# Decay projection of a gated linear attention: one fp32r product over 96 stacked rows instead of one fp32 product over 16

## Chip, cores and metric

The kernel runs on one core of a Trainium2 chip. The metric is the device time of one execution in microseconds. The time before is the median of three runs, 2531.12 us (2529.14 to 2533.62).

## The reference, cut to what matters

A two-layer encoder trunk works on 1040 positions (16 meta tokens and 1024 frames) of width 1024. Each layer has an input projection, a gated linear attention (GLA) with four heads, a softmax attention with a forget gate (FoX) with eight heads, an output projection, and a gated convolutional FFN. The change concerns the per-key decay of the GLA:

```python
gq, gk, gv, gr, glr, fq, fk, fv, ff = jnp.split(xn @ w_in[i], cuts, axis=-1)
log_a = jax.nn.log_sigmoid((glr @ w_alpha_up[i] + b_alpha[i])) / GLA_TAU
...
log_b = jnp.cumsum(log_a, axis=3)          # inside chunks of 64 frames
u = einsum(k * jnp.exp(log_end - log_b), v)  # state increment of a chunk
```

`glr` has 16 columns (the low rank) and `w_alpha_up[i]` is 16 x 256, so the product has a contraction of 16 and gives one decay for each of 4 x 64 keys and each position.

## The kernel before, in words

Activations lie transposed: features on partitions, the 1040 positions along the free axis, which is cut into three chunks of 400, 384 and 256 columns (`CH`).

**Large products.** TensorE is used in fp32r, a 4-byte format of less precision. To keep fp32 accuracy each operand is split into a high part (ScalarE copies it to fp32r) and a low part (VectorE or GpSimd subtracts the high part from the source). `mm3` (L222 to L224) makes a product of three passes: high x high, low weight x high activation, high weight x low activation. Weights are loaded by SP in pieces and split in `weights` (L189 on ScalarE, L191 on VectorE, or on GpSimd in the FoX stage).

**Start of a layer.** `attention` (L886) first makes the GLA. Its head makes three products chunk by chunk: the remainder tile (the 16 low-rank columns in rows 0 to 15, the eight forget-gate columns in rows 32 to 39), the keys `gk` and the first values `gv`. In layer 0 the input is still being split at that time (L297, L298) and squared for the norm (L310 on ScalarE, summed by L311 on VectorE or GpSimd). For each chunk the sum of squares is finished by an fp32 product with ones (L322, `ssq`), and VectorE and ScalarE make the reciprocal root from it (L328, L277, L278, L279 to L281). Then the chunk of the three products is evacuated: `ev_rem` (L909 to L921) adds and scales the remainder tile into `t` (L912 to L914), copies its first 16 rows to `rem` (L915) and makes the log-sigmoid of the forget gates (L346 to L350); `gk` is scaled by L413, the value tiles by L424. After the last chunk the forget gates are summed by a scan (L919) and stored (L921).

**The decay.** When the keys of a pair of heads are complete, `gla_decay` (L455 to L477) is queued behind the next product. For each chunk it makes `z`, an fp32 product of the weights `wau` (16 x 128 of the pair) with 16 rows of `rem` (L462), and its log-sigmoid into the tiles `B` and `A` (L346 to L350). A scan along the chunks (L466), a subtraction from the end of the chunk (L470, L472), an exponential (L476) and a multiplication into the keys (L477) follow. The kernel has two pairs of heads and two layers, so `gla_decay` runs four times, with three `z` products each. `z` uses the PSUM tag `S`, which has three banks; in the head these also hold the products of the third chunk until L413 and L424 evacuate them.

**The steps of the GLA.** `gla_steps` (L480 on) transposes the decayed keys (L491), copies them (`kd`, L492), multiplies them with the values (`u`, L506), updates the states (L513, L515), multiplies the queries with the states (`o`, L523), normalises (L529 to L538, tile `on`) and transposes back (L545). Between these it runs pieces of the next large products (`fill`). The steps of pair 0 run beside the products of pair 1, those of pair 1 beside the first FoX products; `gla_decay` of pair 1 falls into the steps of pair 0. The values are transposed to natural order by `to_natural` (L447, L450).

**Order of the work.** In the attention a scheduler orders the instructions of each engine by its own cost estimates, so a cheaper or an added instruction can move its neighbours. In the FFN the order of TensorE is written out by hand. Every engine takes its own queue in order. GpSimd's queue also issues DMAs, among them the load of `wau` (L904) and the store of the forget gates (L921). Tiles of a pool with the same tag share a buffer: `lc` and `A` share one.

Of the kernel before, what the change touches and what calls it, by code (L numbers as in the profile page):

```python
# [10 lines left out]
F32 = mybir.dt.float32  # L11
F32R = mybir.dt.float32r
BF16 = mybir.dt.bfloat16
AF = mybir.ActivationFunctionType
ALU = mybir.AluOpType
# [6 lines left out]
DEPTH = 2  # L22
META = 16
T = META + SEQ
# [32 lines left out]
class Slots:  # L57
# [6 lines left out]
    def add(self, pool, n, prefix):  # L64
        ids = [(pool, f"{prefix}{i}") for i in range(n)]
        self.free += ids
        return ids
# [68 lines left out]
class Kern:  # L136
# [318 lines left out]
    def gla_decay(self, lyr, p, gp, pp, g):  # L455
        nc = self.nc
        rem, gk = g["rem"], g["gk"]
        A = gp.tile([128, T], F32, tag="A", name="A")
        B = gp.tile([128, T], F32, tag="B", name="B")
        for c0, n in CH:  # L460
            z = pp.tile([128, 512], F32, tag="S", name="z")
            nc.tensor.matmul(z[:, :n], self.wau[:, lyr, 128 * p:128 * p + 128], rem[0:16, c0:c0 + n],  # L462
                             start=True, stop=True)
            self.log_sigmoid(B[:, c0:c0 + n], A[:, c0:c0 + n], z[:, :n], self.v(lyr, V_BA, p),
                             self.ones[:, 0:1])
        nc.vector.tensor_tensor_scan(out=A[:], data0=self.reset[:], data1=B[:], initial=0.0,  # L466
                                     op0=ALU.mult, op1=ALU.add)
        Ar = A[:, META:T].rearrange("p (c t) -> p c t", t=64)
        Br = B[:, META:T].rearrange("p (c t) -> p c t", t=64)
        nc.vector.tensor_tensor(out=Br, in0=Ar[:, :, 63:64].to_broadcast([128, 16, 64]), in1=Ar,  # L470
                                op=ALU.subtract)
        nc.vector.tensor_tensor(out=B[:, 0:META], in0=A[:, META - 1:META].to_broadcast([128, META]),  # L472
                                in1=A[:, 0:META], op=ALU.subtract)
        g["dec"] = dec = gp.tile([128, 16], F32, tag="dec", name="dec", bufs=2)
        nc.scalar.activation(dec[:], Ar[:, :, 63:64].rearrange("p c t -> p (c t)"), AF.Exp, scale=1.0 / 16)
        nc.scalar.activation(B[:], B[:], AF.Exp, scale=1.0 / 16)  # L476
        nc.vector.tensor_tensor(out=gk[:, :T], in0=gk[:, :T], in1=B[:], op=ALU.mult)  # L477
# [408 lines left out]
    def attention(self, lyr, nm, hsrc, chunks, feed):  # L886
        tc, nc, s = self.tc, self.nc, self.slots
        with tc.tile_pool(name=f"aps{lyr}", bufs=2, space=PSUM, reuse_waits="tile") as pp2, \
# [7 lines left out]
            with tc.tile_pool(name=f"gla{lyr}", bufs=1, reuse_waits="tile") as gp:  # L896
                nm["tp"] = gp
                fd = feed(self.wm[lyr, M_REM])
                self.reset = gp.tile([128, T], BF16, name="reset")
                nc.gpsimd.memset(self.reset[:], 1.0)  # L900
                nc.gpsimd.memset(self.reset[:, 0:1], 0.0)
                nc.gpsimd.memset(self.reset[:, META:T].rearrange("p (c t) -> p c t", t=64)[:, :, 0:1], 0.0)
                self.wau = gp.tile([16, DEPTH, 256], F32, name="wau")
                nc.gpsimd.dma_start(self.wau[:], self.wau_d)  # L904
                rem = gp.tile([128, T], F32, tag="rem", name="rem")
                lc = gp.tile([128, T], F32, tag="A", name="lc")
                lr = slice(32, 40)

                def ev_rem(ps, c0, n):  # L909
                    r = self.norm_scale(nm, pp, c0, n)  # L910
                    t = gp.tile([40, 400], F32, tag="rt", name="rt", bufs=2)[:, :n]
                    nc.scalar.copy(t, ps[64:104])  # L912
                    nc.vector.tensor_tensor(out=t, in0=ps[0:40], in1=t, op=ALU.add)
                    nc.vector.tensor_tensor(out=t, in0=t, in1=r[0:40], op=ALU.mult)  # L914
                    nc.scalar.copy(rem[0:16, c0:c0 + n], t[0:16])  # L915
                    self.log_sigmoid(rem[lr, c0:c0 + n], lc[lr, c0:c0 + n], t[lr],
                                     self.v(lyr, V_BF, 0, lr), self.ones[lr, 0:1])
                    if c0 + n == T:
                        nc.vector.tensor_tensor_scan(out=lc[lr, :], data0=self.ones[lr, 0:1].to_broadcast([8, T]),  # L919
                                                     data1=rem[lr, :], initial=0.0, op0=ALU.mult, op1=ALU.add)  # L920
                        nc.gpsimd.dma_start(self.cd[:], lc[lr, :])  # L921
                work = Work()
                add = lambda tiles: [self.add_tile(work, pp, src, nm["x"], CH, ev) for src, ev in tiles]
                g = [{"rem": rem}, {"rem": rem}]
                tiles = [(self.wm[lyr, M_REM], ev_rem)] + self.gla_products(lyr, 0, gp, pp, nm, g[0])
                self.head(tiles[:3], pp, nm, fd)
                if fd:
                    fd["end"]()
                add(tiles[3:])
                work.drain()  # L930
                self.flush()
                add(self.gla_products(lyr, 1, gp, pp, nm, g[1]))
                self.gla_steps(lyr, 0, gp, pp, g[0], lambda us: work.run(us * 1.6))
                work.drain()
                self.flush()
                self.fox_products(lyr, 0, work, gp, pp, nm, qs[0])

                coming = {"src": self.wm[lyr, M_FQ + 1], "slots": None}
                work.boxes.append(coming)
                self.gla_steps(lyr, 1, gp, pp, g[1], lambda us: work.run(us * 1.3))  # L940
                work.drain()
                self.flush()
# [759 lines left out]
def layout(x, meta_tokens, attn_norm, w_in, w_alpha_up, b_alpha, b_forget, gla_norm, fox_norm, w_out,  # L1702
           ffn_norm, w_up, conv_w, conv_b, w_down, final_norm):
    hT0 = np.concatenate([meta_tokens, x[0]], axis=0).T.reshape(KD, 128, T)
    gq, gk, gv, gr, glr, fq, fk, fv, ff = np.split(w_in, np.cumsum([256, 256, 512, 512, 16, 512, 512, 512]), axis=2)
    zero = lambda n: np.zeros((DEPTH, D, n), w_in.dtype)
    rem = np.concatenate([glr, zero(16), ff, zero(88)], axis=2)
    up = w_up.reshape(DEPTH, D, 2, NFF, 128).transpose(0, 1, 3, 2, 4).reshape(DEPTH, D, 2 * NFF * 128)
    cols = np.concatenate([gk, gq, gv, gr, rem, fq, fk, fv, w_out, up], axis=2)
    wm = cols.reshape(DEPTH, KD, 128, N_M, 128).transpose(0, 3, 2, 1, 4)  # L1710
    wd = w_down.reshape(DEPTH, NFF, 128, KD, 128).transpose(0, 3, 2, 1, 4)
    vec = np.zeros((128, V_FIN + 8), w_in.dtype)
    for l in range(DEPTH):
        b = l * NV
        for off, a in ((V_AN, attn_norm[l]), (V_FN, ffn_norm[l]), (V_BA, b_alpha[l]),
                       (V_CW, conv_w[l].reshape(-1)), (V_CB, conv_b[l]), (V_GN, gla_norm[l]),
                       (V_XN, fox_norm[l])):
            t = a.reshape(-1, 128).T
            vec[:, b + off:b + off + t.shape[1]] = t
        vec[32:40, b + V_BF] = b_forget[l]  # L1720
    vec[:, V_FIN:] = final_norm.reshape(KD, 128).T
    wau = w_alpha_up.transpose(1, 0, 2)
    return {"hT0": hT0, "wm": wm, "wd": wd, "vec": vec, "wau": wau}


# [23 lines left out]
```

## Time and profile before

| | |
|---|---|
| median of three runs | 2531.12 us |
| the profiled execution | 2528.19 us |
| its span, first to last instruction | 2526.4 us |
| mean granted TensorE clock | 0.996 |
| `z` products L462 | 12, in 24 records |

A row of the timeline gives the start in us from the span's start, the duration, the engine, the line, the operation with output <- input and shape, the count, and in brackets the idle time of the engine before it and what ended it. A row of the chain of waits gives start, length and what the end of the span was waiting for at that time; there TensorE's instructions stand with the step that they take in its stream. A row of a group gives line, engine, names, shapes and count, then busy us and mean ns of one, then the idle time before them. A row of the waits gives who waited for whom, us in total, times, and the longest. PEld is the load of weights into TensorE.

### The profile page before, as it was taken

What the parts mean: (1) busy time and instruction counts of PE and PEld (TensorE: products, weight loads), DVE (VectorE), ACT (ScalarE), POOL (GpSimd) and SP (SyncE); (2) the same over time, 40 slices, a digit from 0 to 9 for tenths busy, and PEclk for the clock granted to TensorE, in tenths of its full rate; (3) what the DMA queues carried; (4) which work ended last, traced back from release to release, by engine and by line L of the source; (5) the groups of instructions that cost most, each with busy time, mean ns of one, the idle gap of its engine ahead of it and who ended that gap; (6) DMA issues with size and microseconds to landing.
All of it is one profiled execution on the core that took longest, in us unless ns stands there. A gap on an engine that the chain in (4) does not pass through costs nothing.

```text
span 2526.4 us, 47023 instructions
## 1 busy us (share of the span) xinstructions
PE 2488.1 (98%) x18454; PEld 2386.5 (94%) x18454; DVE 1767.5 (70%) x3515; ACT 1274.1 (50%) x2731; POOL 381.4 (15%) x561
## 2 busy tenths in 40 slices
PE   9999999999999999999999999999999999999998
PEld 8989999999999999999999899999999999997786
DVE  8656777769877777853666666777797777777545
ACT  7346666645544445641443466665464444455412
POOL 1023433110000000100200333431100000001002
PEclk9999999999999999999999999999999999999999
DMA  3232124342322224763312222243432222258622
GB/s 131 68 87 73 50 89 132 116 139 76 118 81 81 81 76 138 196 176 102 105 56 70 74 80 69 67 147 110 145 92 93 76 82 83 77 158 191 183 75 73
DMA packets 117933, 259.75 MB, mean 103 GB/s; under 512 B 14816, under 2 KB 32480, under 8 KB 117712
## 3 DMA queue, kind: packets, MB, share of 16 engines
q1 hardware_dynamic: 93408, 181.74, 23.1%
q0 software_dynamic: 22432, 72.71, 10.4%
q8 instruction: 144, 2.36, 0.4%
q10 hardware_dynamic: 1872, 2.31, 0.3%
q14 instruction: 77, 0.63, 0.1%
HBM read 176.11 MB, written 67.81 MB: 97 GB/s over the span
## 4 chain that ended last, share of the span: by engine, by line
PE 83%; DVE 10%; ACT 4%; issue 1%; DMA 1%; SPq 0%; DVEq 0%; ACTq 0%
PE up L224 11%; PE up L222 11%; PE up L223 11%; PE mm L222 7%; PE mm L224 7%; PE mm L223 7%; PE down L222 5%; PE down L223 5%; PE down L224 5%; PE av L721 3%; PE tr L695 2%; DVE S L662 1%; PE S L659 1%; PE wo L222 1%; PE wo L224 1%
## 5 line engine op out<-in xcount | busy, mean ns | idle before, releaser
L224 PE MATMUL up<-x,hi 128*128 128x260 f32 (+1 forms) x2464 | 698.0, 283 | 2.8 <-DVE x L1090 2.8
L222 PE MATMUL up<-x,hi 128*128 128x260 f32 (+1 forms) x2464 | 698.2, 283 | 2.4 <-ACT x L1089 2.4
L223 PE MATMUL up<-x,lo 128*128 128x260 f32 (+1 forms) x2464 | 697.1, 283 | 0.0
L224 PEld LDWEIGHTS up<-x,hi 128*128 128x128 f32 x2464 | 466.8, 189 | 5.1 <-DVE x L1090 4.8
L222 PEld LDWEIGHTS up<-x,hi 128*128 128x128 f32 x2464 | 465.7, 189 | 3.3 <-ACT x L1089 3.2
L223 PEld LDWEIGHTS up<-x,lo 128*128 128x128 f32 x2464 | 466.0, 189 | 0.1
L1066 DVE TENSOR_TENSOR lo<-raw,hi 128x512 fp32r<-128x512 f32 x364 | 247.5, 685 | 172.0 <-ACT hi L1065 172.0
L222 PE MATMUL mm<-xh,hi 128*128 128x348 f32 (+4 forms) x1056 | 363.6, 344 | 0.0
L224 PE MATMUL mm<-xl,hi 128*128 128x348 f32 (+4 forms) x1056 | 339.6, 322 | 0.0
L223 PE MATMUL mm<-xh,lo 128*128 128x348 f32 (+4 forms) x1056 | 338.9, 321 | 0.0
L1065 ACT CAST hi<-raw 128x512 fp32r<-128x512 f32 x364 | 224.8, 620 | 141.5 <-PE up L224 93.0
L222 PEld LDWEIGHTS mm<-xh,hi 128*128 128x128 f32 x1056 | 199.6, 189 | 5.9 <-issue 5.3
L223 PEld LDWEIGHTS mm<-xh,lo 128*128 128x128 f32 x1056 | 199.5, 189 | 0.4 <-issue 0.3
L224 PEld LDWEIGHTS mm<-xl,hi 128*128 128x128 f32 x1056 | 198.4, 188 | 0.4 <-issue 0.3
L189 ACT CAST hi<-raw 128x512 fp32r<-128x512 f32 (+2 forms) x168 | 97.3, 580 | 183.2 <-PE down L224 108.0
L223 PE MATMUL down<-ah,lo 128*128 128x260 f32 (+1 forms) x528 | 169.1, 320 | 0.0
L222 PE MATMUL down<-ah,hi 128*128 128x260 f32 (+1 forms) x528 | 168.6, 319 | 0.0
L224 PE MATMUL down<-al,hi 128*128 128x260 f32 (+1 forms) x528 | 168.4, 319 | 0.0
L674 ACT ACTIVATE P<-S,m 116x460 f32<-116x460 f32 (+2 forms) x224 | 124.7, 561 | 71.6 <-DVE m L662 67.6
L337 DVE TENSOR_TENSOR PT<-tr,PT 116x464 fp32r<-116x464 f32 (+3 forms) x240 | 122.8, 514 | 47.0 <-ACT PT L336 45.4
L1048 DVE TENSOR_TENSOR raw<-raw,raw 128x512 f32<-128x512 f32 x198 | 129.4, 683 | 18.1 <-DMA raw<-in_wd_dram 15.6
L1279 POOL DMA_DIRECT2D actd<-cv x44 | 23.6, 535 | 763.0 <-DVE cv L1278 742.1
(285 smaller groups left out, 5615.6 us busy)
## 6 DMA issues: line engine op xcount, KB each, us to landing
raw<-in_wm_dram SPq DMA_DIRECT2D x326, 256.0 KB, 2.7
raw<-in_wd_dram SPq DMA_DIRECT2D x64, 256.0 KB, 3.8
actd<-cv POOLq DMA_DIRECT2D x22, 520.0 KB, 3.0
actd<-cv POOLq DMA_DIRECT2D x22, 512.0 KB, 3.0
cb<-cd SPq DMA_DIRECT2D x16, 520.0 KB, 4.2
st<-actd SPq DMA_DIRECT2D x14, 520.0 KB, 5.0
st<-actd SPq DMA_DIRECT2D x14, 512.0 KB, 4.8
kA<-kA SPq DMA_DIRECT2D x24, 260.0 KB, 4.1
```

Of the source, the lines that this page charges most:

```text
L189: nc.scalar.copy(hi[:, :n, :], raw[:, :n, :])
L222: nc.tensor.matmul(ps, wh, xh[:, c0:c0 + n], start=first, stop=False, skip_group_check=more)
L223: nc.tensor.matmul(ps, wl, xh[:, c0:c0 + n], start=False, stop=False, skip_group_check=more)
L224: nc.tensor.matmul(ps, wh, xl[:, c0:c0 + n], start=False, stop=last, skip_group_check=more)
L337: nc.vector.tensor_tensor(out=lo, in0=src, in1=hi.bitcast(F32), op=ALU.subtract)
L659: nc.tensor.matmul(S[:rows, :n], q["qA"][e][:, qs], q["kA"][e][:, c0:k1], start=True, stop=False)
L674: nc.scalar.activation(P[:rows, :n], S[:rows, :n], AF.Exp, scale=-1.0, bias=m[:rows, nch - 1:nch], accum_out=(den if nch == 1 else d3[:row ...
L695: nc.tensor.transpose(tr[:w, 3 - j, :rows], P[:rows, o:o + w], id_)
L721: nc.tensor.matmul(av[:, a:b], w.rearrange("p a b -> p (a b)"), x, start=(t == ts[0] and part == 0 and i == 0), stop=(t == last and i == 1))
L1048: nc.vector.tensor_tensor(out=q[out][:, :nk, :], in0=q[a][:, :nk, :], in1=q[b][:, :nk, :], op=op)
L1065: nc.scalar.copy(hi[:, :nk, :], src[:, :nk, :])
L1066: nc.vector.tensor_tensor(out=lo[:, :nk, :], in0=src[:, :nk, :], in1=hi[:, :nk, :].bitcast(F32), op=ALU.subtract)
```

## The change

The product `z` keeps its shape and its place, and becomes a single fp32r product with a contraction of 96 rows. The rows are three groups of 32, of which 16 carry data: activations high, low, high, and weights high, high, low. One pass so adds the same three terms as `mm3`.

- `ev_rem` writes the three groups of `rz`: the high part by ScalarE (32 rows in place of 16), the low part by a subtraction on VectorE, the second copy of the high part by GpSimd.
- The host layout of `wau` holds the weights three times in 96 rows, and a layer loads its own part only. After the last chunk ScalarE copies the 96 x 256 weights to fp32r (`wz`), and VectorE replaces the last group by its low part.
- The forget gates keep their tile `rem`, which now shares the buffer of tag `B`; `rz` takes the buffer of tag `rem`.

```diff
@@ gla_decay
-            nc.tensor.matmul(z[:, :n], self.wau[:, lyr, 128 * p:128 * p + 128], rem[0:16, c0:c0 + n],
-                             start=True, stop=True)
+            nc.tensor.matmul(z[:, :n], self.wz[:, 128 * p:128 * p + 128], rem[:, c0:c0 + n], start=True, stop=True)
@@ attention
-                self.wau = gp.tile([16, DEPTH, 256], F32, name="wau")
-                nc.gpsimd.dma_start(self.wau[:], self.wau_d)
-                rem = gp.tile([128, T], F32, tag="rem", name="rem")
+                wau = gp.tile([96, 256], F32, name="wau")
+                nc.gpsimd.dma_start(wau[:], self.wau_d[:, lyr, :])
+                self.wz = wz = gp.tile([96, 256], F32R, name="wz")
+                rz = gp.tile([96, T], F32R, tag="rem", name="rz")
+                rem = gp.tile([128, T], F32, tag="B", name="rem")
...
-                    nc.scalar.copy(rem[0:16, c0:c0 + n], t[0:16])
+                    hi, lo, hi2 = (rz[a:a + 32, c0:c0 + n] for a in (0, 32, 64))
+                    nc.scalar.copy(hi, t[0:32])
+                    nc.vector.tensor_tensor(out=lo, in0=t[0:32], in1=hi.bitcast(F32), op=ALU.subtract)
+                    nc.gpsimd.tensor_copy(hi2, hi.bitcast(F32))
...
                         nc.gpsimd.dma_start(self.cd[:], lc[lr, :])
+                        nc.scalar.copy(wz[:], wau[:])
+                        nc.vector.tensor_tensor(out=wz[64:96, :], in0=wau[64:96, :], in1=wz[64:96, :].bitcast(F32),
+                                                op=ALU.subtract)
...
-                g = [{"rem": rem}, {"rem": rem}]
+                g = [{"rem": rz}, {"rem": rz}]
@@ layout
-    wau = w_alpha_up.transpose(1, 0, 2)
+    wau = np.zeros((96, DEPTH, 256), w_in.dtype)
+    for a in (0, 32, 64):
+        wau[a:a + 16] = w_alpha_up.transpose(1, 0, 2)
```

In the changed kernel the new lines are L917 (high part), L918 (low part), L919 (second copy), L926 and L927 (weights); the scan of the forget gates is L923, and lines of `gla_decay` and `gla_steps` stand one lower than before (L462 keeps its number). The prediction names lines that both kernels have by their number before.

## The prediction

> **What bounds the kernel now.** I read the page first: span, busy shares, clock, chain.
>
> ```profile
> span 2526.4 us, 47023 instructions
> PE 2488.1 (98%) x18454; PEld 2386.5 (94%) x18454; DVE 1767.5 (70%) x3515; ACT 1274.1 (50%) x2731; POOL 381.4 (15%) x561
> PEclk9999999999999999999999999999999999999999
> GB/s 131 68 87 73 50 89 132 116 139 76 118 81 81 81 76 138 196 176 102 105 56 70 74 80 69 67 147 110 145 92 93 76 82 83 77 158 191 183 75 73
> PE 83%; DVE 10%; ACT 4%; issue 1%; DMA 1%; SPq 0%; DVEq 0%; ACTq 0%
> ```
>
> TensorE is busy for 98% of the span at the full granted clock, and 83% of the chain is its own work. So a microsecond taken from its stream is a microsecond off the end, unless another engine makes it wait at that place. The second view is therefore TensorE's waits. The place near the change that already waits is the products u of the GLA steps, for the transposed keys kd (0.9 us in two waits, one in each layer):
>
> ```profile
> PE u L506 <- DVE kd L492: 0.9, 2, 0.5
> ```
>
> The third view is the chain of waits cut to the places where the decay product z (L462) stands. It gives each instruction its real step in TensorE's stream, while the matmul durations of other views overlap each other. There are four sets of z: GLA pair 0 and pair 1, in each of two layers; each has three chunks (400, 384 and 256 columns).
>
> ```profile
> 47.16 0.18 PE mm L222
> 47.70 1.72 PE z L462 x4
> 49.44 0.67 PE z L462 x2
> 50.11 0.37 PE tr L450 x2
> 50.83 0.17 PE mm L224
> 89.66 1.94 PE z L462 x6
> 1301.38 1.94 PE z L462 x6
> 1310.11 0.12 PE mm L222
> 1342.92 1.94 PE z L462 x6
> ```
>
> The sets last 2.41 us (layer 0, pair 0: 47.70 to 50.11) and 1.94 us (the three others). A chunk is two records, since it is an fp32 product. The fp32r products beside them take one record and 0.18, 0.17 and 0.12 us for 400, 384 and 256 columns. The first set is longer because it waits inside:
>
> ```profile
> 48.52 0.29 PEld L462 LDWEIGHTS z<-rem,wau 16*128 16x128 f32 x2 [0.59 <-DVE gk L413]
> 49.41 0.29 PEld L462 LDWEIGHTS z<-rem,wau 16*128 16x128 f32 x2 [0.60 <-ACT lc L346]
> ```
>
> The second chunk waits for the evacuation of gk (L413) and the third for that of the first value tile (L424): z takes the PSUM banks that those free. In layer 0 VectorE's queue, and not TensorE, already sets the end of this set.
>
> **The change, part by part.**
>
> *TensorE, removed and added.* Twelve fp32 products become twelve fp32r products with 96 rows; the rows of a contraction do not lengthen it: the steps above are of products with 128 rows. A set then costs 0.18 + 0.17 + 0.12 = 0.47 us; I take 0.50, since entering another kind of product costs some hundredths. An unhindered set falls from 1.94 to 0.50: **1.44 us** saved. Four of them would be 5.8 us.
>
> *What the order of the built program says.* On SP the order is the same. On TensorE, VectorE and ScalarE it differs only in the GLA stage of each layer; the FoX and FFN stages are unchanged instruction for instruction. So nothing else needs pricing but the two GLA stages. Four kinds of work are added per layer: three subtractions L918 and one L927 on VectorE, one copy L926 on ScalarE (256 columns, 0.4 us by L915 below, and ScalarE is busy for half of the span), three copies L919 on GpSimd. L917 takes the place of L915 with twice the rows and the same columns.
>
> *Layer 0, pair 0.* VectorE's queue decides here. Its rows:
>
> ```profile
> 37.95 1.23 DVE L191 TENSOR_TENSOR lo<-raw,hi 128x512 fp32r<-128x512 f32 x1
> 39.10 0.54 DVE L281 SCALAR_TENSOR_TENSOR r<-ra,y 128x384 f32<-128x384 f32 x1
> 39.67 0.55 DVE L914 TENSOR_TENSOR rt<-rt,r 40x384 f32<-40x384 f32 x1
> 42.08 0.69 DVE L191 TENSOR_TENSOR lo<-raw,hi 128x512 fp32r<-128x512 f32 x1
> 43.02 0.42 DVE L913 TENSOR_TENSOR rt<-mm,rt 40x256 f32<-40x256 f32 x1 [0.25 <-ACT rt L912]
> 43.66 0.55 DVE L350 TENSOR_TENSOR rem<-rem,lc 8x384 f32<-8x384 f32 x1 [0.23 <-ACT lc L348]
> 44.91 0.42 DVE L328 TENSOR_SCALAR vv<-ssq 128x256 f32<-128x256 f32 x1
> 47.71 0.42 DVE L914 TENSOR_TENSOR rt<-rt,r 40x256 f32<-40x256 f32 x1
> 48.06 0.41 DVE L413 TENSOR_TENSOR gk<-mm,r 128x256 f32<-128x256 f32 x1
> 48.50 0.34 DVE L349 TENSOR_SCALAR rem<-rt,vec 8x256 f32<-8x256 f32 x1
> 48.87 0.90 DVE L424 TENSOR_TENSOR vt<-mm,r 128x256 f32<-128x256 f32 x2
> ```
>
> A subtraction of 32 rows is priced by L914, 40 rows of the same length: a step of 0.48 us at 400 and 384 columns, 0.38 at 256. Ahead of L281 come L918 (0.48) and L927 (0.4), and one L191 leaves (1.15, the slow one): L281 of the second chunk stays at about 39.1. Between it and L328 of the third chunk come L918 (0.48) and that L191 at its undisturbed step (0.61), 1.09 in all. The two waits on ScalarE (0.25 and 0.23) absorb 0.48 of it, and another 0.16 goes to smaller gaps: L328 starts about 0.45 late, at 45.36. From there the chain keeps its steps to L349, then L918 (0.38) stands ahead of L424. The first L424 ended near 49.37 (its pair is 0.90 from 48.87, and the third z loads at 49.41); now it ends near 49.37 + 0.45 + 0.38 = 50.20. The last z then ends at 50.20 + 0.05 + 0.12 = 50.37 in place of 50.11. **This set loses 0.25 us**: all that TensorE saves is given back to the wait. Waits of TensorE further ahead (xl of the third chunk and vt of the second each come later on VectorE) end before this one and are absorbed by it. Bounds: 0.3 gained if VectorE loses nothing up to L328, 1.1 lost if none of the added work finds slack.
>
> The third way to z is the GpSimd copy, which is not in the trace. It starts when the high part is there, which in layer 0 is 0.45 later than the end of L915 was:
>
> ```profile
> 48.16 0.40 ACT L915 COPY rem<-rt 16x256 f32<-16x256 f32 x1 [1.93 <-DVE rt L914]
> 1300.30 0.41 ACT L915 COPY rem<-rt 16x256 f32<-16x256 f32 x1 [1.93 <-DVE rt L914]
> L573 POOL TENSOR_TENSOR qA<-qt,qA 64x348 fp32r<-64x348 f32 x32 | 29.8, 933 | 25.7 <-ACT qA L572 24.0
> L839 POOL TENSOR_TENSOR cb<-cb,mask 116x116 f32<-116x116 f32 x128 | 58.8, 461 | 213.2 <-DVE m L662 152.9 <-DMA cb<-cd 26.9 <-DVE fa L279 11.5
> ```
>
> Its nearest rows are 0.46 us (116 columns, two inputs) and 0.93 (348 columns, two inputs); for 256 columns and one input I take 0.65, an estimate between them. It lands at 48.56 + 0.45 + 0.05 + 0.65 = 49.7, before 50.20, and costs nothing here; at 0.93 it still lands before it. The first copy (400 columns) stands in GpSimd's queue ahead of seven additions for the norm, the last five of which are these, with TensorE's ssq product that reads them:
>
> ```profile
> 34.09 4.54 POOL L311 TENSOR_TENSOR r<-r,sq 128x256 f32<-128x256 f32 x5 [0.78 <-ACT sq L310]
> 42.90 0.43 PE ssq L322 x2
> ```
>
> They end at 38.63 and are read at 42.90, so they have 4 us to spare and that copy is hidden.
>
> *Layer 1, pair 0.* VectorE has idle time ahead of this set, so only the last additions count:
>
> ```profile
> 1301.01 0.98 DVE L424 TENSOR_TENSOR vt<-mm,r 128x256 f32<-128x256 f32 x2
> 1303.32 0.37 PE tr L450 x2
> ```
>
> L918 pushes the first L424 from 1301.46 to 1301.84. GpSimd's copy ends at 1300.71 + 0.05 + 0.65 = 1301.4 (1301.7 at 0.93). The first two z take 1301.38 to 1301.78, the third starts at 1301.9 and ends at 1302.07, against 1303.32. **1.25 us gained** (0.6 to 1.45).
>
> *Pair 1, both layers.* The operands are old, so z itself waits for nothing and TensorE runs 1.44 us ahead. But it runs towards the wait for kd:
>
> ```profile
> 96.00 0.56 DVE vt L424
> 96.56 2.23 DVE A L466
> 100.78 0.48 DVE kd L492
> 101.30 0.89 PE u L506 x24
> ```
>
> TensorE came to u at 100.85 and waited 0.45. The new order puts seven 400-column products and one transpose (7 x 0.18 + 0.11 = 1.39 us) ahead of u, so TensorE comes to u at 100.80. On VectorE the new order is denser before the scan L466 (both L538 and all of L350 now stand ahead of it): counting steps from the first L349 I get the scan at 96.5 and kd at 101.6, against 101.26. Then u starts at 101.65, 0.35 later but with 1.39 more done: **1.05 us gained** in each layer. Bounds: 0.4 if kd slips by another 0.65, 1.9 if kd is there when TensorE comes.
>
> *Start.* The load of wau grows from 32 to 96 KB in layer 0, beside the loads on which the first products wait. At the 131 GB/s of the first slice, 64 KB are 0.5 us if they all stood in the way; I take 0.1.
>
> **Sum.** -0.25 + 1.25 + 2 x 1.05 - 0.1 = 3.0 us. The profiled execution took 2528.19 us (span 2526.4 and 1.8 around it); it would take 2525.2. The median of the runs shown is 2531.12, 2.9 above it, so I forecast 2531.1 - 3.0 = **2528.1 us**, 0.12% faster. A measurement of this kernel can tell about 0.2%, or 5.1 us, from no change, so this counts as within.
>
> **Rivals.**
>
> *A: the whole saving arrives.* kd is ready when TensorE comes, so the old waits go too (1.9 per layer), layer 1 pair 0 gives 1.4 and layer 0 nothing: 5.2 us, 2525.9. For it: the scan no longer stands behind the vt evacuation that TensorE released at 96.0. Against it: by my count VectorE is busy without a gap from 90.6 to 101.6. It decides from kd being 0.8 us earlier than I count.
>
> *B: GpSimd holds up VectorE, and the kernel is slower.* The trace shows the same L191 at 1.23 us beside GpSimd's additions and at 0.69 without them, so a copy on GpSimd can cost VectorE time. If each L919 costs VectorE its whole length at the high price (0.93), the three in layer 0 delay L424 by up to 2.8 us and the last in layer 1 by 0.9: 3.0 - 3.7 = -0.7, 2531.8. It decides from 0.75 us of delay per copy, four copies eating 3.0 us. Against it: two of the copies meet VectorE at work that reads PSUM or one small operand, and L191 lost 0.54 beside some five additions in a row.
> The Trainium skill (SBUF — State Buffer, Who interferes with whom) says that a VectorE instruction with two SBUF inputs contends with a GpSimd instruction that reads SBUF, and that the lock is held for the whole instruction. The 1.23 beside 0.69 agrees in direction; L918 has two SBUF inputs and L919 reads SBUF, so by that rule B is the case, with L918 of the third chunk waiting out its L919.
>
> *C: the fp32r product is no faster here* (96 rows in three groups, each half padded with zeros). Then only the added work is left: 0.25 + 0.4 + 0.1, about 2532. Against it stands every fp32r row above.
>
> **Chances.** Forecast 0.58, A 0.25, B 0.12, C 0.05. Most of A, and about one in seven of the forecast (scatter of a median: the runs shown go from 2529.1 to 2533.6), end faster by over 0.2%: 0.30. Part of B and C, where several delays meet, end slower by over 0.2%: 0.08. The rest, 0.62, lies within. Range: from the best ends of the terms (0.3 + 1.45 + 3.8 = 5.5 us gained, and 2 us of scatter) to the worst (-1.1 + 0.6 + 0.8 - 0.5 = -0.2, and 1.2 of scatter): 2523.6 to 2532.5.
>
> **What would show it.** Right: the z sets on the chain are 0.5 us in pair 1; the third z of pair 0 in layer 0 still waits on L424 near 50.2; u still waits for kd, 0.5 to 0.9 us; everything after the GLA stages keeps its durations and is only earlier. Wrong: z steps above 0.2 us (C); L918 or L191 much longer beside L919 (B); no wait at u (A); z waiting on GpSimd in layer 1; or a new TensorE wait at the transposes of on (L545 before), which I count at nothing because VectorE reaches them within 0.3 us.

## The result and the profile after

The changed kernel takes 2527.09 us (median of 22 runs, 2524.9 to 2531.38) against 2531.12 (22 runs, 2528.36 to 2535.32). The ratio is 0.9983 with a 95% interval of 0.9977 to 0.9989: some 4.3 us or 0.17% less, within the 0.2% that the prediction took as the bound of what a measurement can tell. Two more sets of 11 runs of the changed kernel, taken beside the experiments, gave 0.9987 (0.9978 to 0.9995) and 0.9988 (0.9979 to 0.9997). So there is a gain. The three intervals have 2.8 to 5.3 us in common, and the stages below give 2.0 to 3.5.

The page of the changed kernel, in the lines that answer to those of before. The last line is from TensorE's waits over the whole span (us in total, times, longest).

```profile
span 2528.4 us, 47014 instructions
PE 2483.1 (98%) x18442; PEld 2385.4 (94%) x18442; DVE 1771.4 (70%) x3523; ACT 1274.4 (50%) x2733; POOL 385.0 (15%) x567
PEclk9999999999999999999999999999999999999999
...
PE 78%; DVE 14%; ACT 5%; issue 2%; DMA 1%; SPq 0%; DVEq 0%; ACTq 0%
...
PE u L505 <- DVE kd L491: 0.8, 2, 0.4
```

TensorE has 12 instructions less and 5.0 us less to do, but VectorE holds 14% of the chain in place of 10%. The profiled execution took 2530.31 us, 2.1 more than the profiled one of before, while the medians differ by 4.0 the other way. One execution of each can't be subtracted as a whole: by the table below the stages with the change gained 2 us even in this execution, and the rest of the difference arises in stages that the change doesn't touch.

So the comparison is made by stage. Each product in one trace is paired with the same product in the trace of before (same line and tiles, same count), and the starts are subtracted. That offset is flat for long stretches and steps where one kernel waits or works longer. The table gives its step across each set of z (median over products behind the set, less median ahead of it), in us, with minus for a gain. "Half clock" says whether the granted clock fell to 0.50 inside the stage.

| kernel | layer 0 pair 0 | layer 0 pair 1 | layer 1 pair 0 | layer 1 pair 1 | sum | half clock | ratio by runs (95%) |
|---|---|---|---|---|---|---|---|
| predicted | +0.25 | -1.05 | -1.25 | -1.05 | -3.1 | | |
| changed, first profile | +2.17 | -1.62 | -1.00 | -1.59 | -2.04 | layer 0 pair 0 | 0.9983 (0.9977 to 0.9989) |
| changed, second | +0.71 | -1.64 | -1.01 | -1.58 | -3.52 | no | 0.9987 (0.9978 to 0.9995) |
| changed, third | +0.69 | -1.63 | -1.01 | -1.59 | -3.53 | no | 0.9988 (0.9979 to 0.9997) |
| high parts only, 16 rows | -0.97 | -1.22 | -1.28 | -1.05 | -4.52 | no | 0.9984 (0.9975 to 0.9993) |
| high parts only, 96 rows | -1.06 | -1.64 | -1.52 | -1.43 | -5.65 | no | 0.9976 (0.9966 to 0.9986) |
| added work only, z as before | +1.65 | -0.05 | -0.01 | +1.54 | +3.13 | layer 1 pair 1 | 1.0012 (1.0002 to 1.0021) |
| low parts on GpSimd, copies on ScalarE | -0.34 | -1.61 | -1.52 | -1.59 | -5.06 | no | 0.9976 (0.9967 to 0.9985) |
| first chunk off VectorE | +2.11 | -1.64 | -1.08 | -1.59 | -2.19 | layer 0 pair 0 | 0.9984 (0.9975 to 0.9993) |
| copies on ScalarE | +0.82 | -1.61 | -1.09 | -1.59 | -3.47 | no | 0.9979 (0.9970 to 0.9988) |
| first low part twice | +2.66 | -1.61 | -1.01 | -1.59 | -1.54 | layer 0 pair 0 | 0.9989 (0.9980 to 0.9998) |
| nearly all on GpSimd | -0.13 | -1.62 | -1.52 | -1.59 | -4.85 | no | 0.9978 (0.9969 to 0.9987) |

Three of the four sets repeat within 0.1 us from profile to profile. Outside these sets the offsets of the same traces wander by up to 4 us. The intervals of the runs are some 4 to 5 us wide for 11 runs, so the stages tell more here than the medians.

The sets of z in the changed kernel, from TensorE's timeline (start, time, instruction, what it was idle for). Rows overlap, so the time of a set is from its first row to the start of the next other row.

```profile
52.22 0.36 PE L462 MATMUL z<-rz,wz 96*128 96x256 f32 x1 [0.34 <-DVE vt L424]
52.41 0.39 PE L450 MATMUL tr<-ident,vt 128*128 128x128 f32 x2
...
91.83 0.63 PE L462 MATMUL z<-rz,wz 96*128 96x400 f32 x3
92.30 0.34 PE L222 MATMUL mm<-xh,hi 128*128 128x384 f32 x1
...
1303.76 0.36 PE L462 MATMUL z<-rz,wz 96*128 96x256 f32 x1 [0.37 <-DVE vt L424]
```

An unhindered set takes 0.47 us (91.83 to 92.30) in place of 1.94. In pair 0 of both layers the third chunk waits for the first L424 of the 256 columns, and not for GpSimd.

What the prediction did not have is ahead of the first set. VectorE's timeline, TensorE's waits from 20 to 150 us, and the windows of 3 us (busy time of TensorE, its weight loads, VectorE, ScalarE, GpSimd; then the granted clock):

```profile
30.93 0.57 DVE L424 TENSOR_TENSOR vt<-mm,r 128x400 f32<-128x400 f32 x1
31.54 0.56 DVE L918 TENSOR_TENSOR rz<-rt,rz 32x400 fp32r<-32x400 f32 x1
...
33.91 1.13 DVE L350 TENSOR_TENSOR rem<-rem,lc 8x400 f32<-8x400 f32 x1
...
36.73 1.08 DVE L279 SCALAR_TENSOR_TENSOR ra<-y 128x384 f32<-128x384 f32 x1
37.73 0.94 DVE L298 SCALAR_TENSOR_TENSOR xl<-hin,vec,xh 128x256 fp32r<-128x256 f32 x1
...
47.16 0.42 DVE L328 TENSOR_SCALAR vv<-ssq 128x256 f32<-128x256 f32 x1 [1.46 <-PE ssq L322]
...
51.65 0.90 DVE L424 TENSOR_TENSOR vt<-mm,r 128x256 f32<-128x256 f32 x2
```

```profile
PE mm L388 <- DVE xl L298: 1.7, 2, 1.5
```

```profile
36.00:39.00 3.00, 1.28 (x9) 0.88 (x7) 3.00 (x4) 2.31 (x6) 2.23 (x3) 0.95 0.00 0
39.00:42.00 3.00, 3.00 (x16) 3.00 (x16) 2.91 (x7) 0.70 (x2) 0.08 (x1) 0.50 0.09 12
42.00:45.00 3.00, 3.00 (x26) 3.00 (x26) 2.94 (x7) 2.55 (x5) 0.51 (x1) 0.98 0.23 81
```

L918 of the first chunk (0.56 us) stands ahead of the last values xl of the third chunk (L298), L350 takes 1.13 us where it took 0.56 (it now runs beside GpSimd's additions L311, which start at 33.87), and in the new order L279 (a step of 1.00) comes ahead of the last L298 too. TensorE waits 1.7 us for it. In this execution the granted clock then falls to 0.50 for 0.3 + 3.0 + 0.12 = 3.4 us (from the three windows: twice the missing share of each). The sums of squares come late, and now VectorE waits 1.46 us for TensorE at L328.

### The profile page after: what moved, and what is told of

It reads as the page before. It is cut to its first block, busy times and chain, and to the rows that moved or that the text cites. A ratio compares the mean times of both kernels' runs of the same rounds, so it can differ in the third digit from the quotient of the medians.

```text
span 2528.4 us, 47014 instructions
## 1 busy us (share of the span) xinstructions
PE 2483.1 (98%) x18442; PEld 2385.4 (94%) x18442; DVE 1771.4 (70%) x3523; ACT 1274.4 (50%) x2733; POOL 385.0 (15%) x567
## 4 chain that ended last, share of the span: by engine, by line
PE 78%; DVE 14%; ACT 5%; issue 2%; DMA 1%; SPq 0%; DVEq 0%; ACTq 0%
PE up L224 10%; PE up L222 10%; PE up L223 10%; PE mm L222 7%; PE mm L223 7%; PE mm L224 7%; PE down L222 5%; PE down L223 5%; PE down L224 5%; PE av L720 3%; PE tr L694 2%; DVE S L661 2%; DVE x L1097 1%; ACT P L673 1%; PE S L658 1%
```

## The experiments

The first theory: this wait, with the half clock behind it, is what layer 0 loses, and VectorE's added work makes it. Rivals: the loss is scatter of one execution; it needs the new products and not the added work; GpSimd's copies make it.

**The changed kernel again** (no edit).

> The changed kernel once more. Theory (the stall is the kernel's own): L918 of the first chunk and what it pushes stand ahead of the last L298 on VectorE, so TensorE again waits 1 to 2 us for xl near 37 to 39 us, the granted clock is again near 0.50 in the window 39:42, and the first z set of layer 0 ends about 2.2 us later against the stream than before; time about 4 us below before. Rival (scatter of one execution): no wait over 0.5 us at that place, granted clock 1.00, the first z set within 0.5 us of before's place.

The wait for xl came back to the digit. The clock did not fall, so this half of the expectation was a miss.

```profile
36.00:39.00 3.00, 1.28 (x9) 1.09 (x10) 2.94 (x6) 1.79 (x4) 1.63 (x2) 1.00 0.00 0
39.00:42.00 3.00, 3.00 (x28) 3.00 (x26) 2.92 (x7) 1.35 (x3) 0.60 (x1) 1.00 0.24 68
```

TensorE is idle for the same 1.7 us of the first window, and then goes on at full clock. The set loses 0.71 us and not the 2.2 that I expected. So the wait is the kernel's own; the half clock is a matter of the execution, and it is worth 1.46 us.

**High parts only.**

```diff
-z: self.wz[:, ...], rem[:, c0:c0 + n]
+z: self.wz[0:16, ...], rem[0:16, c0:c0 + n]
-L918, L919, L927
```

> The decay projection as one fp32r product of the 16 high rows only: L918, L919 and L927 are gone, so the low parts are left out of the result of z. Theory (the added VectorE work makes the stall in layer 0): no wait for xl at 37 to 39 us, clock 1.00 in 39:42, the first set of layer 0 at about its old place or 0.3 us earlier, layer 1 pair 0 1.4 us and each pair 1 about 1.6 us earlier; about 3 us below the changed kernel, some 7 below before. Rival (the additions are hidden and the stall comes from TensorE's new order): stall stays, time as the changed kernel. Rival (96 rows cost more than 16): z steps here are shorter than 0.18, 0.17, 0.12 us.

No wait for xl, clock 1.00, and layer 0 pair 0 gains 0.97 us, three times what I had expected without the added work. But the pair-1 sets gained only 1.22 and 1.05, less than in the changed kernel: the product of 16 rows is slower than that of 96.

```profile
88.87 0.74 PE L462 MATMUL z<-rz,wz 16*128 16x400 f32 x3
89.53 0.45 PE L222 MATMUL mm<-xh,hi 128*128 128x384 f32 x1
```

The set takes 0.66 us here (88.87 to 89.53) against 0.47 with 96 rows. The expectation of 3 us below the changed kernel was a miss: by the stages it is 1.0 (4.52 against 3.52), by the runs no difference shows.

**Added work only.**

```diff
-z: self.wz (fp32r, 96 rows), rz fp32r
+z: self.wau[0:16, ...] (fp32, 16 rows), rz fp32; L917, L918, L919, L926, L927 kept
```

> All the added work (L917 to L919, L926, L927) is issued, but z stays the fp32 product of 16 rows, so nothing is saved on TensorE. Theory: the stall for xl near 37 to 39 us and the half clock come back, layer 0 pair 0 ends about 2.2 us late, the other sets lose 0 to 0.4 us: about 3 us above before (2534). Rival (the stall needs the fp32r products): no stall, time within 0.5 us of before. Rival B (GpSimd's copies hold up VectorE): in layer 1 the first L424 is late by 0.6 us or more.

The wait for xl is there (1.7 us), and the kernel is slower by 0.12% (0.02 to 0.21%), 3.0 us by the ratio, 3.13 by the stages. So the added work does it by itself. GpSimd's copies don't show as rival B had it: in layer 1 the first L424 starts 0.51 us late against TensorE's stream, which is no more than the low part ahead of it takes (0.50), and not 0.6 or more. But the sum is made up in another way than expected: layer 0 pair 0 loses 1.65 at full clock, and 1.54 are lost in layer 1 pair 1, where TensorE waited for nothing new and the clock fell all the same:

```profile
1348.00:1352.00 4.00, 4.00 (x16) 4.00 (x16) 3.75 (x13) 3.21 (x9) 0.00 (x0) 0.59 0.00 0
```

**Low parts on GpSimd, second high copies on ScalarE.**

```diff
-nc.vector.tensor_tensor(out=lo, ...)        (L918; L927 alike)
+nc.gpsimd.tensor_tensor(out=lo, ...)
-nc.gpsimd.tensor_copy(hi2, hi)              (L919)
+nc.scalar.copy(hi2, t[0:32])
```

> The whole change, but VectorE gets none of its work: the low parts L918 and L927 go to GpSimd, and the second high copy L919 goes to ScalarE. Theory (VectorE's queue is what costs in layer 0): the stall for xl and the half clock go, the first set of layer 0 is within 0.5 us of before's place, and the time is about 3 us below the changed kernel. Rival B (work on GpSimd holds up VectorE by the shared access, or GpSimd is too late for the third z): the third z of pair 0 waits for L918 on GpSimd, or L350 and L191 grow by 0.5 us each, and the time is that of the changed kernel or above.

The wait for xl is gone and with it the half clock, layer 0 pair 0 gains 0.34 us, layer 1 pair 0 the full 1.52. The ratio is 0.9976. GpSimd now sets the third z of layer 0, as the rival had it, but at a price that leaves a gain (waits of TensorE from 20 to 150 us):

```profile
PE z L462 <- DVE gk L413: 0.7, 1, 0.7
PE z L462 <- POOL rz L918: 0.5, 1, 0.5
```

**First chunk off VectorE.** The next question is which part of the added work it is. Here only the first chunk's low part goes to GpSimd and its copy to ScalarE.

```diff
-nc.vector.tensor_tensor(out=lo, ...)
+(nc.vector if c0 else nc.gpsimd).tensor_tensor(out=lo, ...)
-nc.gpsimd.tensor_copy(hi2, hi)
+(nc.gpsimd if c0 else nc.scalar) copy
```

> Only the first chunk's low part goes to GpSimd and its second high copy to ScalarE; the other two chunks stay as in the changed kernel. In the built program the last L298 of the third chunk then stands before L279 again. Theory (the first chunk's L918 and the order that it brings make the whole stall): no wait for xl at 37 us, and the first set of layer 0 loses only what L918 of the other two chunks and L927 cost, 0.2 to 0.7 us against before instead of the 0.7 and 2.2 seen with the stall; time at or up to 0.8 us below the changed kernel. Rival (any low part on VectorE in layer 0 costs as much): the set loses 0.7 us or more with another wait in its place.

The wait for xl is gone, as expected, and the loss is not: 2.11 us. In its place TensorE waits at z itself (waits, then windows):

```profile
PE z L462 <- DVE vt L424: 0.9, 1, 0.9
PE z L462 <- DVE gk L413: 0.9, 1, 0.9
```

```profile
51.00:54.00 3.00, 3.00 (x14) 3.00 (x13) 2.68 (x2) 0.37 (x1) 0.00 (x0) 0.64 0.00 0
54.00:57.00 3.00, 3.00 (x17) 2.92 (x16) 0.04 (x1) 0.00 (x0) 0.55 (x1) 0.79 0.09 11
```

Two waits of 0.9 us, and again the half clock for 2 x (0.36 + 0.21) x 3 = 3.4 us. Less the 1.46 that this cost above, the set loses 0.65: about the same as with the wait for xl. (The trace shows it directly too: the products right behind z are 0.61 us late, and 2.1 once the half clock is over.) The theory that the wait for xl is the loss falls here. The wait as such costs nothing; it is taken out of the later wait of z, as the prediction had said. What is lost at full clock, 0.7 us, is set by the end of VectorE's queue at L424.

**Copies on ScalarE.** Only L919 is moved.

```diff
-nc.gpsimd.tensor_copy(hi2, hi)
+nc.scalar.copy(hi2, t[0:32])
```

> The second high copies L919 go to ScalarE; the low parts L918 stay on VectorE. In the built program the last L298 comes before L279, but still behind L918. Theory (the stall is L918 0.6 us, the place behind L279 1.0 us, and L350 0.57 us longer beside GpSimd, less 0.9 us that there was to spare): the wait for xl shrinks from 1.7 us to 0 to 0.6 us and the first set of layer 0 loses 0.2 to 0.9 us; about the time of the first-chunk run. Rival (L918's own length alone makes it): the wait stays at 1.2 us or more. Rival B (GpSimd's copy holds VectorE): L350 is back at 0.56 us and the wait is gone.

The wait for xl is gone and L350 is back at 0.56, as rival B had it: that wait hangs on the copies, or on the order that they bring. But the set loses 0.82 us, as much as the changed kernel at full clock, so the loss doesn't hang on them alone. It doesn't clear them either: here ScalarE has the copies to do, and L927 takes 0.85 us in place of 0.42. What a copy on GpSimd can cost L918 of the second chunk, which takes 0.55 us here, shows in the kernel with the first chunk off VectorE, by VectorE's and GpSimd's timelines:

```profile
41.24 0.74 DVE L918 TENSOR_TENSOR rz<-rt,rz 32x384 fp32r<-32x384 f32 x1
```

```profile
40.99 0.59 POOL L920 CAST rz<-rz 32x384 fp32r<-32x384 f32 x1 [1.68 <-ACT rz L917]
```

The copy and L918 overlap for 0.34 us (41.24 to 41.58), and L918 takes 0.19 longer. The Trainium skill (SBUF — State Buffer, SBUF: two separate sides) says that whichever of the two starts first has the shared ports for its whole instruction. By that L918 would be 0.34 us longer: the direction agrees, and the measured 0.19 is less.

**First low part twice.**

```diff
+for _ in range(1 if c0 else 2): L918
```

> L918 of the first chunk is issued twice in each layer (the second writes the same values). Theory: the wait for xl grows by the 0.6 us of one L918 to 2.3 us, and the granted clock falls to 0.50 for 3 us behind it, as it did in one of three runs with a wait of 1.7 us; the first set of layer 0 loses 1.3 us (clock kept) to 2.8 us (clock halved); time 0.6 to 2.1 us above the changed kernel. Rival (the stall is absorbed by the later wait of z): the set's loss stays at 0.7 us.

The wait for xl grew only to 1.9 us and not to 2.3; the order shifted again. The clock fell, and the set loses 2.66 us, 1.2 without the fall.

```profile
39.00:42.00 3.00, 2.95 (x18) 2.95 (x19) 2.94 (x6) 0.40 (x1) 0.00 (x0) 0.70 0.00 0
42.00:45.00 3.00, 3.00 (x21) 3.00 (x20) 2.86 (x7) 2.85 (x6) 0.59 (x1) 0.73 0.30 93
```

Here too the half clock lasts 2 x (0.30 + 0.27) x 3 = 3.4 us.

**High parts only, 96 rows.** The rows 32 to 95 are zeros, set once per layer.

```diff
-L918, L919, L927
+nc.gpsimd.memset(rz[32:64], 0), nc.gpsimd.memset(rz[64:96], 0)
```

> The fp32r product over all 96 rows, but rows 32 to 95 of its input are zero and set once per layer by GpSimd, so that L918, L919 and L927 are left out (z lacks the low parts). Theory (the product of 16 rows paid 0.10 us on entry and 0.08 us on exit that the one of 96 rows does not): an unhindered set takes 0.47 us here against 0.66 us with 16 rows; no stall; gains of 0.3, 1.6, 1.4 and 1.6 us in the four sets, 4.9 us in all. Rival (the entry cost comes from what the set follows, not from its rows): 0.66 us again, 4.3 us in all.

```profile
88.51 0.63 PE L462 MATMUL z<-rz,wz 96*128 96x400 f32 x3
88.98 0.34 PE L222 MATMUL mm<-xh,hi 128*128 128x384 f32 x1
```

The set is back at 0.47 us, so the 0.19 us more of the 16 rows come from the rows and not from the place. The products beside the set are faster too: from the 128-row product ahead of z to the second one behind it TensorE takes 0.83 us here (88.32 to 89.15) and 1.23 with 16 rows (88.59 to 89.82). The four sets gain 5.65 us, where I had expected 4.9 (the first gained 1.06 and not 0.3): this is what TensorE's part of the change is worth without the low parts and the second copies. The changed kernel gives back 5.65 - 3.52 = 2.1 us of it to the added work, 1.75 in layer 0 pair 0 and 0.5 in layer 1 pair 0, less 0.15 in layer 1 pair 1.

**Nearly all on GpSimd**, to get that back, and **the changed kernel a third time** beside it.

```diff
-L918, L927 on VectorE; L926 on ScalarE
+L918, L927, L926 on GpSimd; L919 on GpSimd, of the last chunk on ScalarE
```

> The whole change with no work of it on VectorE and little on ScalarE: all low parts (L918), the first two second high copies and the preparation of the weights go to GpSimd; only the last chunk's second high copy goes to ScalarE. Theory (in the run with the copies on ScalarE, that engine made VectorE wait 0.32 and 0.16 us ahead of L328 and so kept the first set of layer 0 at a gain of 0.3 us): that set now gains 0.6 to 1.0 us against before, near the 1.06 us of the run without low parts, the other three 1.6, 1.5 and 1.6 us; 5.5 us in all, 2525.4. Rival (GpSimd's two-input work holds VectorE up, or is itself late): rows of VectorE at 0.98 us in place of 0.55 through 40 us, the set gains 0.3 us or less or waits for L918 or for the sums of squares; 4.8 us in all or less.

> The changed kernel a third time, for the granted clock behind its wait for xl and to stand beside the other two on one chip. Theory: the wait of 1.7 us and its place are the same; the first set of layer 0 loses 0.7 us if the clock in 39:42 is 1.00 and 2.2 us if it is 0.50, nothing between; time 3 to 4.5 us below before. Rival (the stall's own length sets the loss): 2.2 us with the clock at 1.00.

The first is a miss: layer 0 pair 0 gains 0.13 and not 0.6 to 1.0, and the rival is right. VectorE's two-input work beside a busier GpSimd is longer:

```profile
34.01 0.99 DVE L350 TENSOR_TENSOR rem<-rem,lc 8x400 f32<-8x400 f32 x1
...
38.71 1.22 DVE L191 TENSOR_TENSOR lo<-raw,hi 128x512 fp32r<-128x512 f32 x1
```

L350 takes 0.99 in place of 0.56, and L191 takes 1.22, as it did before beside GpSimd's additions, where an undisturbed one takes 0.69. By the stages this kernel gains 4.85 us, where the rival had 4.8 or less. The third profile of the changed kernel lost 0.69 us with the clock at 1.00, as that theory said; its VectorE rows stand in the next section.

Of all the kernels with the full computation, the one with the low parts on GpSimd and the copies on ScalarE has the largest gain by the stages (5.06 us) and the lowest ratio (0.9976). It ran beside the second set of the changed kernel, and the medians of these two sets of 11 runs are 2524.83 and 2527.64, 2.8 us apart; drawing the runs again at random puts this between 0.8 and 4.5 (95%). So it is faster than the changed kernel, by the runs and by the stages (5.06 against 3.52).

## Why the prediction was right, point by point

The time was right (2528.1 forecast, 2527.1 measured), partly because errors of its terms cancel: 3.0 us forecast, 3.5 by the stages at full clock, 2.0 in the profile with the half clock.

- **The set of z, 0.50 us.** Right: 0.47, and 96 rows cost no more than 128. The entry cost that I allowed for is absent with 96 rows and there with 16.
- **Layer 0, pair 0, a loss of 0.25 us.** Right in mechanism (the third z waits for L424; VectorE's queue gives all of TensorE's gain back), wrong in size: 0.70. The term that was mis-sized is L918. VectorE's timeline before, and in the third profile of the changed kernel, which reached L424 of the first chunk 0.21 us later:

```profile
30.74 0.57 DVE L424 TENSOR_TENSOR vt<-mm,r 128x400 f32<-128x400 f32 x1
...
33.62 0.56 DVE L350 TENSOR_TENSOR rem<-rem,lc 8x400 f32<-8x400 f32 x1
```

```profile
30.95 0.57 DVE L424 TENSOR_TENSOR vt<-mm,r 128x400 f32<-128x400 f32 x1
31.55 0.56 DVE L918 TENSOR_TENSOR rz<-rt,rz 32x400 fp32r<-32x400 f32 x1
32.15 0.85 DVE L298 SCALAR_TENSOR_TENSOR xl<-hin,vec,xh 128x256 fp32r<-128x256 f32 x1
...
42.49 0.55 DVE L918 TENSOR_TENSOR rz<-rt,rz 32x384 fp32r<-32x384 f32 x1
43.05 0.56 DVE L424 TENSOR_TENSOR vt<-mm,r 128x384 f32<-128x384 f32 x1
...
45.74 0.43 DVE L328 TENSOR_SCALAR vv<-ssq 128x256 f32<-128x256 f32 x1
...
49.71 0.50 DVE L918 TENSOR_TENSOR rz<-rt,rz 32x256 fp32r<-32x256 f32 x1
50.22 0.91 DVE L424 TENSOR_TENSOR vt<-mm,r 128x256 f32<-128x256 f32 x2
```

  The steps of L918 are 0.60, 0.56 and 0.51 us, not the 0.48, 0.48 and 0.38 that I took from L914. L328 is 0.62 late (45.74 - 0.21 - 44.91; I had 0.45) and L424 1.14 (50.22 - 0.21 - 48.87; I had 0.83). These 0.31 are most of the 0.45 us that were missing; another 0.07 is the last z, which takes 0.19 ahead of the transposes (52.22 to 52.41 in the first profile) where I had 0.12. The rest is not located.
- **"Waits of TensorE further ahead ... are absorbed by it."** This sentence failed, though only in part. The wait for xl, 1.7 us, is absorbed: without it the set loses as much. But a wait can also bring the half clock, and that is absorbed by nothing: 1.46 us in the profile in which it did. I had read the clock as a constant of the page, 9 in every slice.
- **Layer 1, pair 0, 1.25 us.** 1.00. The third z waits for L424 as predicted, which L918 holds up by 0.51 in place of 0.38; that is 0.13 of the 0.25 that were missing, and the rest is not located.
- **Pair 1, 1.05 us each.** 1.6. I had kd later than it is. The chain of the first profile:

```profile
91.99 0.20 PE z L462
...
98.36 2.23 DVE A L465
...
102.86 0.48 DVE kd L491
103.38 0.89 PE u L505 x24
```

  This set starts 2.33 us later than before (91.99 against 89.66). Less that, the scan starts at 96.03, and I had 96.5; u starts at 101.05, and I had 101.65. TensorE still waits 0.4 us for kd, as predicted, but no longer than before, so the 1.39 us of other products ahead of u are all gained, and about 0.2 more (by the prediction's own rounded terms, 7 x 0.18 + 0.11, these products are 1.37). TensorE's part was also mis-sized: from the 128-row product ahead of z to the second one behind it, it takes 2.49 us before (89.32 to 91.81) and 0.83 after (91.64 to 92.47). So a set saves 1.66 and not 1.44, because the 16-row products also hold up the products beside them.
- **The start, 0.1.** Not resolved: the offset there lies between -0.5 and +0.5 us in the traces of the changed kernels, which all load the same 96 KB.
- **Rival A** is nearer in size for pair 1 (1.9 there, 1.6 measured, 1.05 forecast) and wrong in mechanism: the wait at u stayed.
- **Rival B** did not come as put: the third z never waited longer for L919 than for L424. But a small part of it is there. GpSimd's copy of the third chunk in the third profile, and VectorE's L918 of that chunk in the kernel with the copies on ScalarE:

```profile
49.47 0.47 POOL L919 CAST rz<-rz 32x256 fp32r<-32x256 f32 x1 [6.94 <-ACT rz L917]
```

```profile
49.86 0.41 DVE L918 TENSOR_TENSOR rz<-rt,rz 32x256 fp32r<-32x256 f32 x1
```

  Beside the copy L918 takes 0.50 us (49.71 above), without it 0.41. That is 0.09 of the 0.13 by which its last step was mis-sized, and layer 1 pair 0 gains 0.08 more where the copies are on ScalarE (1.09 against 1.01). Beside two-input work on GpSimd VectorE loses more, as the rows of L350 and L191 show.
- **Rival C** is out by the 0.47. Its price was wrong as well: its 0.25 for the first set is what is left after TensorE's saving, which C denies. With z as before, the added work cost 1.65 us in that set, and nothing in layer 1 pair 0 (the prediction had 0.4).

What stays open: why the clock fell in layer 1 pair 1 of the kernel with the added work only, where TensorE was never idle. Why the same wait of 1.7 us brought the half clock in one of four profiles (three of the changed kernel, and the one with the added work only) is answered for the most part by the grid in the last section.

## What to carry to other kernels

When a saving on TensorE is paid for on another engine, price the addition in the stage where that engine's queue ends last; elsewhere it is free. Here the saving was 5.65 us without the added work. It arrived whole in two sets of four, while instructions of 0.4 to 0.6 us on VectorE ate more than all of one set and a third of another. And compare small changes by the offset between the two instruction streams, stage by stage: it settled differences of 0.1 us where the runs of a kernel spread over 6.

## What the runs showed of the hardware

**The granted clock falls in pieces of 3.4 us.** The page rounds it away, but windows of 4 us over the whole trace of before show it:

```profile
456.00:460.00 4.00, 3.02 (x20) 3.02 (x21) 4.00 (x16) 4.00 (x12) 1.08 (x2) 0.80 0.12 35
460.00:464.00 4.00, 4.00 (x28) 3.96 (x28) 3.87 (x12) 4.00 (x13) 0.57 (x1) 0.78 0.52 164
612.00:616.00 4.00, 3.64 (x19) 3.64 (x20) 4.00 (x8) 0.35 (x1) 0.88 (x1) 0.58 0.42 131
```

At 456 to 464 it is 2 x (0.20 + 0.22) x 4 = 3.4 us again. Leaving out the last microseconds of each trace, there are four such pieces in this one (456, 612, 1708 and 1864 us), one in that of the kernel with the copies on ScalarE (1860), and three to six in the others. At about 1.5 us each they go with the scatter of the runs: over the 129 runs behind the rows of the table above, each set taken against its own mean, the time and the mean granted clock correlate at -0.69.

**The clock is decided on a fixed grid.** By the clock's record in the trace of before, the falls begin at 458.37, 611.97, 1711.06 and 1864.66 us. These are 45, 322 and 45 times 3.413 us apart, and in every other trace too the falls lie on such a grid, to 0.01 us. So each trace can be cut into windows of 3.413 us that end where a fall can begin. TensorE's idle time in these windows, by its busy time in them, around the waits of layer 0:

| kernel | windows (us) | idle (us) | clock behind |
|---|---|---|---|
| changed, first profile | 35.30:38.71 | 1.71 | 0.50 |
| changed, second | 33.55:36.96, 36.96:40.38 | 0.64, 1.08 | 1.00 |
| changed, third | 33.79:37.20, 37.20:40.61 | 0.17, 1.53 | 1.00 |
| added work only | 33.74:37.15, 37.15:40.56 | 0.43, 1.27 | 1.00 |
| first low part twice | 33.37:36.79, 36.79:40.20 | 0.42, 1.49 | 0.50 |
| first chunk off VectorE | 48.42:51.83 | 1.75 | 0.50 |

The same wait of 1.7 us was followed by a fall where one window held all of it, and by none where two windows shared it. Over all twelve traces (some 8800 windows, without the first 8 and the last 14 us) a fall came behind all 22 windows with 1.75 us or more of idle time, behind 15 of the 26 with 1.38 to 1.75, and behind 2 of all others. So about half a window of idle time is where it turns; what decides between 1.38 and 1.75 is not shown, and one of the last two falls came behind a window without any idle time (1344.46:1347.87 in the kernel with the added work only). The Trainium skill (TensorE: Matmul & The Clock Gate, Part 1: The HAM clock gate) says that the clock follows an activity window of about 3.4 us that runs freely, and falls after an idle window of that length. The length and the free running agree. The condition doesn't: half of such a window was enough.

**A product of 16 rows between products of 128 costs more than one of 96**: 0.66 us against 0.47 for a set of three, and 1.23 against 0.83 with the products beside it, which is the 0.4 us by which the pair-1 sets differ in the stages (1.22 against 1.64, 1.05 against 1.43). The Trainium skill (TensorEngine Tiling (Array Packing), Key Properties) says that a change of tiling mode drains TensorE. That fits, if the 16 rows are such a mode; no run here shows it directly.
